# Loads of the second layer's modulation strips, moved from SyncE's queue to ScalarE's

## The chip, the cores and the metric

One core of a Trainium2 chip runs the whole program. The time is the device time of one execution in microseconds (us). The kernel before takes 1233.61 us (median of three runs, 1233.14 to 1236.70).

In the profile's rows PE is the matrix engine (TensorE), PEld its weight loads, DVE VectorE, ACT ScalarE, POOL GpSimd, SP SyncE. A name with a q behind it (SPq, ACTq) is the engine's instruction queue, where DMAs are begun.

## The reference, cut to what matters

Two decoder layers on 512 tokens of width 1024. Every layer computes six modulation vectors from one conditioning vector, and uses them as shift, scale and gate:

```
cond = jax.nn.silu(c)
for layer in range(DEPTH):
    mod = cond @ ada_w[layer] + ada_b[layer]
    sh1, sc1, g1, sh2, sc2, g2 = jnp.split(mod, 6, axis=-1)
    h = modulate(rms_norm(x, mix_norm[layer]), sh1, sc1)
    ...                                    # the layer's mixer gives y
    x = x + g1[:, None, :] * y
    h = modulate(rms_norm(x, ffn_norm[layer]), sh2, sc2)
    x = x + g2[:, None, :] * swiglu(h, ffn_w1[layer], ffn_w2[layer])
```

The second layer's mixer is a pooling mixer over four windows beside a stick-breaking attention of four heads; one output projection follows. `sh2` and `sc2` of that layer (strips 3 and 4 of its `ada_w`, each 1024 x 1024) are needed only behind the mixer, and the kernel computes them during it.

## The kernel before, in words

**The strips.** `ada_strip` (lines 249 to 265; an earlier identical definition is overwritten) walks one strip in four quarters of 256 columns. A quarter is two loads of 512 KB (line 258) into the two `ada` tiles (the pool has two), then sixteen small matmuls (line 247, eight per tile) and a copy of the sum from PSUM into half of an accumulator tile `acc` (line 264, on ScalarE). It is a generator that yields once between the loads of a quarter and its matmuls. So one step of it does: matmuls of quarter k, copy k, then the two loads of quarter k+1, which need the tiles that matmuls k have just read. Strips 3 and 4 of layer 1 give eight quarters, called pair 1 to 8 (loads), product 1 to 8 (matmuls) and copy 1 to 8 below. Copies 1, 3, 5 and 7 are the first to write a new `acc` tile; 2, 4, 6 and 8 fill the other half of one.

**The mixer's order.** `run` (lines 559 to 566) advances one main generator of twenty steps, `l1_main`, and after each of its steps one step of the side generators and then one of the strips. The first step traces the start of the attention's key projection; then `fin1` traces the broadcast of a gate (`gate_bcast`, two copies at line 380), then pair 1 is traced. Product k comes in step k+1. Attention (`sbatt`) starts in step 7: `stA` of head 0 in step 7 (with product 6), `stA` of head 1 in step 8 (ahead of product 7), `stB` of head 0 in step 9 (ahead of product 8). `stA` of a head takes twelve heap tiles: `sz`, `sa`, `sphi` and `splo`, three each.

**What sets the order of instructions.** In this stretch TensorE keeps program order, by `manual_schedule`. On the other engines a planner orders instructions while the program is built: it runs the program in a simulation and takes what is ready, earlier in the program first. Two further rules matter. `tc.keep_in_program_order` pins an instruction behind the instruction traced last before it on its own engine, in issue order alone. And tiles of a pool get their buffers in program order: the heap has 52 slots of 2 KB per partition, shared by `acc`, the pooling's and the attention's tiles, and in the program of before every one of the 970 heap tiles is begun in the order in which the program writes them first, so an instruction that begins a heap tile is not placed before those that begin earlier ones.

**Queues.** Loads of weights (`raw`, 1 MB each, lines 439 and 452, two buffers) are begun by SyncE, as are all loads of strips. ScalarE begins a load of `pool_w` (line 1714) and small ones.

Of the kernel before, what the change touches and what calls it, by code (L numbers as in the profile page):

```python
# [69 lines left out]
def trunk(ctx, tc, x, c, positions, ada_w, ada_b, ffn_w1, ffn_w2, ab_w_in, gla_gate_up,  # L70
          dsa_q_norm, dsa_k_norm, ab_w_out, cd_w_in, pool_w, cd_w_out, prm, w0, kc, out):
    nc = tc.nc
# [24 lines left out]
    def slot(dt=F32, w=512, name="s"):  # L97
        return heap.tile([P, w], dt, tag="s", name=nm(name))

    def bank(name="b"):  # L100
        return pp.tile([P, 512], F32, tag="b", name=nm(name))
# [4 lines left out]
    def ada_tile():  # L106
        return adap.tile([P, 1024], F32, tag="ada", name=nm("ada"))
# [98 lines left out]
    def ada_mm(ps, rows, j0, j1):  # L206

        for j in range(j0, j1):
            g = j % 4
            mm(ps[32 * g:32 * g + 32, :], condz[:, j, :], rows[j], start=j < 4, stop=j >= 4)  # L210

    def ada_strip(l, s, acc2, lag):
        src = ada_w[l].rearrange("(p j) n -> p j n", j=8)
        for n in range(2):
            acc = slot(name="acc")
            for q in range(2):
                c0 = s * D + n * 512 + q * 256
                rows = []
                for h in range(2):
                    rt = ada_tile().rearrange("p (j n) -> p j n", j=4)  # L220
                    tc.keep_in_program_order(nc.sync.dma_start(rt, src[:, 4 * h:4 * h + 4, c0:c0 + 256]))
                    rows += [rt[:, j] for j in range(4)]
                for _ in range(lag):
                    yield
                ps = bank("ad")
                ada_mm(ps[:, 0:256], rows, 0, 8)
                act(acc[:, q * 256:(q + 1) * 256], ps[:, 0:256], AF.Copy)
            acc2.append(acc)
# [17 lines left out]
            g = j % 4  # L246
            mm(ps[32 * g:32 * g + 32, :], condz[:, j, :], rows[j], start=j < 4, stop=j >= 4)  # L247

    def ada_strip(l, s, acc2, lag):
        src = ada_w[l].rearrange("(p j) n -> p j n", j=8)  # L250
        for n in range(2):
            acc = slot(name="acc")
            for q in range(2):
                c0 = s * D + n * 512 + q * 256
                rows = []
                for h in range(2):
                    rt = ada_tile().rearrange("p (j n) -> p j n", j=4)
                    tc.keep_in_program_order(nc.sync.dma_start(rt, src[:, 4 * h:4 * h + 4, c0:c0 + 256]))
                    rows += [rt[:, j] for j in range(4)]
                for _ in range(lag):  # L260
                    yield
                ps = bank("ad")
                ada_mm(ps[:, 0:256], rows, 0, 8)
                act(acc[:, q * 256:(q + 1) * 256], ps[:, 0:256], AF.Copy)
            acc2.append(acc)
# [293 lines left out]
    def run(main, *sides, keep=()):  # L559
        live = [iter(g) for g in sides]  # L560
        for _ in main:
            live = [g for g in live if next(g, "end") != "end"]
            for g in keep:
                next(g, None)
        while live:
            live = [g for g in live if next(g, "end") != "end"]

    def delay(g, n):
        for _ in range(n):
            yield  # L570
        yield from g
# [9 lines left out]
    def chain(*gens):  # L581
        for g in gens:
            yield from g
# [594 lines left out]
    for s_ in (2, 3, 4):  # L1178
        ada0[s_] = []
    ad = delay(chain(*(ada_strip(0, s_, ada0[s_], 1) for s_ in (2, 3, 4))), 2)  # L1180
    next(sst)
    lo_eng[0] = nc.gpsimd
# [350 lines left out]
    ada1 = {s_: [] for s_ in range(2, 6)}  # L1533
# [214 lines left out]
    def fin1():  # L1748
        gl["g1"] = gate_bcast(ada1[2])
        yield  # L1750

    def l1_main():
        yield from in_cd()
        yield from outproj_first(cd_w_out[0], 0, mixC, gl["g1"])

    lo_eng[0] = nc.gpsimd
    ad = chain(*(ada_strip(1, s_, ada1[s_], 1) for s_ in (3, 4)))
    run(l1_main(), fin1(), delay(sbatt(), 6), keep=(ad,))
    for _ in ad:
        pass  # L1760
# [37 lines left out]
```

## Time and profile before

| | us |
|---|---|
| median of three runs | 1233.61 |
| lowest, highest | 1233.14, 1236.70 |
| the profiled execution | 1229.25 |
| its span, first to last instruction | 1227.5 |
| PE busy in it | 1199.4 (98%) |
| ACT busy in it | 591.2 (48%) |
| mean granted TensorE clock | 0.993 |

The profiled execution is 4.4 us below the median of the timed runs; 1.75 us of it lie outside its span. The second layer's mixer with its strips lies at about 690 to 860 us of the span. A row of a timeline is: start us, us (from the first instruction's start to the last one's end where several are merged), engine, line, operation, output<-input, count, and in brackets the engine's idle time just before with what ended it. A queue's row is the same for begun DMAs.

### The profile page before, as it was taken

To read this page: it belongs to the slowest core of one execution; us is meant where nothing else is said; L and a number is where in the kernel's file an instruction comes from. 1 tells how busy PE (TensorE), PEld (TensorE's weight loads), DVE (VectorE), ACT (ScalarE), POOL (GpSimd) and SP (SyncE) were. 2 spreads that over 40 slices of the span, in tenths; PEclk is the share of its full clock that TensorE was granted. 3 is DMA by queue.
4 is the path that set the end of the run, shared out by engine and by line. 5 is a ranking of instruction groups with operands and counts; after the bars stand their busy time and mean duration, and the time that the engine had idled before them with its cause. 6 is when DMAs were issued, how large, how long until landed. Compare 5 with 4: busy or idle time off the path is not lost.

```text
span 1227.5 us, 19275 instructions
## 1 busy us (share of the span) xinstructions
PE 1199.4 (98%) x7584; PEld 1039.1 (85%) x7584; DVE 893.8 (73%) x1478; ACT 591.2 (48%) x1125; POOL 154.1 (13%) x153
## 2 busy tenths in 40 slices
PE   7998999999999999999999999999999999999998
PEld 3776777878899999998887877787899999998886
DVE  4487799667798787879786726765898878778333
ACT  5366347645465555553232763652465555553231
POOL 2133135500100000000000263140100000000000
PEclk8998999999999999999999999999999999999999
DMA  9544554321123423228972356322224242235221
GB/s 324 202 137 162 165 190 141 135 89 39 37 99 104 136 78 130 89 84 283 258 283 103 104 171 211 108 69 69 69 70 138 76 132 86 87 131 213 103 69 68
DMA packets 112662, 160.87 MB, mean 131 GB/s; under 512 B 7078, under 2 KB 77750, under 8 KB 112572
## 3 DMA queue, kind: packets, MB, share of 16 engines
q1 hardware_dynamic: 110544, 158.72, 39.0%
q8 instruction: 59, 0.97, 0.3%
q10 hardware_dynamic: 1964, 0.93, 0.3%
q14 instruction: 31, 0.25, 0.1%
q0 software_dynamic: 64, 0.01, 0.0%
HBM read 157.53 MB, written 2.10 MB: 130 GB/s over the span
## 4 chain that ended last, share of the span: by engine, by line
PE 83%; DVE 7%; DMA 4%; ACT 2%; issue 2%; POOL 1%; SPq 0%; ACTq 0%; DVEq 0%; POOLq 0%
PE f L1430 11%; PE f L1427 11%; PE f L1429 11%; PE f L123 4%; PE w L124 4%; PE f L124 4%; PE w L125 4%; PE f L125 4%; PE w L123 4%; PE op L124 2%; PE op L125 2%; PE op L123 2%; DMA raw<-in_ffn_w_dram 2%; PE ad L247 2%; PE f L131 2%
## 5 line engine op out<-in xcount | busy, mean ns | idle before, releaser
L119 ACT ACTIVATE whi<-raw 128x1024 fp32r<-128x1024 f32 x164 | 171.8, 1056 | 199.3 <-PE w L125 91.3
L120 DVE TENSOR_TENSOR wlo<-raw,whi 128x1024 fp32r<-128x1024 f32 x124 | 151.2, 1222 | 88.8 <-ACT whi L119 88.8
L1430 PE MATMUL f<-hhi,wlo 128*128 128x256 f32 x640 | 181.3, 283 | 0.0
L1429 PE MATMUL f<-hlo,whi 128*128 128x256 f32 x640 | 181.3, 283 | 0.0
L1427 PE MATMUL f<-hhi,whi 128*128 128x256 f32 x640 | 181.3, 283 | 0.0
L124 PE MATMUL w<-wlo,ghi 128*128 128x512 f32 x352 | 137.4, 390 | 0.5 <-DVE wlo L120 0.4
L123 PE MATMUL w<-whi,ghi 128*128 128x512 f32 x352 | 137.4, 390 | 0.3 <-ACT ghi L119 0.3
L125 PE MATMUL w<-whi,glo 128*128 128x512 f32 x352 | 137.2, 390 | 0.0
L1429 PE MATMUL f<-tlo,whi 128*128 128x256 f32 x480 | 136.0, 283 | 0.0
L1427 PE MATMUL f<-thi,whi 128*128 128x256 f32 x480 | 136.0, 283 | 0.0
L1430 PE MATMUL f<-thi,wlo 128*128 128x256 f32 x480 | 136.0, 283 | 0.0
L1434 ACT ACTIVATE e<-f 128x512 f32<-128x512 f32 x100 | 59.7, 597 | 138.9 <-PE f L1430 138.8
L1427 PEld LDWEIGHTS f<-hhi,whi 128*128 128x128 f32 x640 | 123.0, 192 | 0.0
L1429 PEld LDWEIGHTS f<-hlo,whi 128*128 128x128 f32 x640 | 123.0, 192 | 0.0
L1430 PEld LDWEIGHTS f<-hhi,wlo 128*128 128x128 f32 x640 | 123.0, 192 | 0.0
L120 POOL TENSOR_TENSOR wlo<-raw,whi 128x1024 fp32r<-128x1024 f32 x40 | 97.5, 2446 | 162.4 <-ACT whi L119 144.4
L120 DVE TENSOR_TENSOR wlo<-s,whi 128x512 fp32r<-128x512 f32 (+1 forms) x100 | 76.1, 794 | 43.9 <-ACT whi L119 43.9
L123 PE MATMUL f<-whi,hhi 128*128 128x512 f32 x240 | 96.7, 403 | 1.8 <-DVE iqr L771 1.8
L124 PE MATMUL f<-wlo,hhi 128*128 128x512 f32 x240 | 94.8, 395 | 0.1
L125 PE MATMUL f<-whi,hlo 128*128 128x512 f32 x240 | 94.4, 393 | 0.0
L1429 PEld LDWEIGHTS f<-tlo,whi 128*128 128x128 f32 x480 | 92.2, 192 | 0.0
L1430 PEld LDWEIGHTS f<-thi,wlo 128*128 128x128 f32 x480 | 92.2, 192 | 0.0
(341 smaller groups left out, 2547.8 us busy)
## 6 DMA issues: line engine op xcount, KB each, us to landing
raw<-in_ffn_w_dram SPq DMA_DIRECT2D x54, 1024.0 KB, 5.1
ada<-in_ada_w_dram SPq DMA_DIRECT2D x42, 512.0 KB, 5.2
ar<-in_ada_w_dram SPq DMA_DIRECT2D x68, 256.0 KB, 5.9
raw<-in_ab_w_in_dram SPq DMA_DIRECT2D x12, 1024.0 KB, 5.1
ada<-in_ffn_w_dram SPq DMA_DIRECT2D x24, 512.0 KB, 3.7
ar<-in_ada_w_dram SPq DMA_DIRECT2D x64, 128.0 KB, 4.0
raw<-in_cd_w_in_dram SPq DMA_DIRECT2D x8, 1024.0 KB, 5.1
x<-in_x_dram SPq DMA_DIRECT2D x16, 256.0 KB, 5.0
```

The costliest lines, as they stand in the source:

```text
L119: act(hi, src, AF.Copy)
L120: lo_eng[0].tensor_tensor(lo, src, hi, op=ALU.subtract)
L123: mm(ps, ah, bh, start=first, stop=False)
L124: mm(ps, ah, bl, start=False, stop=False)
L125: mm(ps, al, bh, start=False, stop=last)
L131: mm(ps, ah, bh, start=i == 0, stop=False)
L247: mm(ps[32 * g:32 * g + 32, :], condz[:, j, :], rows[j], start=j < 4, stop=j >= 4)
L1427: mm(ps, hi[:, k, c_], bh, start=start and k == 0 and p == 0, stop=False, skip_group_check=not start or p == 1)
L1429: mm(ps, hi[:, k, c_], bl, start=False, stop=False, skip_group_check=not start or p == 1)
L1430: mm(ps, lo[:, k, c_], bh, start=False, stop=k == 3, skip_group_check=not start or p == 1)
L1434: act(ends[name], src, fn)
```

## The change

The strip generator gets an argument that names the engine which begins its loads. For the two strips that run in the second layer's mixer it is ScalarE; the first layer's strips keep SyncE. Sixteen loads of 512 KB are concerned. Since the pin works on the load's own engine, each pair is now pinned behind the instruction traced last on ScalarE: pair 1 behind the second copy of the gate (line 380), and pair k+1 behind copy k (line 264). On SyncE the weight loads and the strips' loads no longer stand in one order.

```
-    def ada_strip(l, s, acc2, lag):
+    def ada_strip(l, s, acc2, lag, eng=nc.sync):
...
-                    tc.keep_in_program_order(nc.sync.dma_start(rt, src[:, 4 * h:4 * h + 4, c0:c0 + 256]))
+                    tc.keep_in_program_order(eng.dma_start(rt, src[:, 4 * h:4 * h + 4, c0:c0 + 256]))
...
-    ad = chain(*(ada_strip(1, s_, ada1[s_], 1) for s_ in (3, 4)))
+    ad = chain(*(ada_strip(1, s_, ada1[s_], 1, nc.scalar) for s_ in (3, 4)))
```

## Rows read from the trace of the kernel before

**Rows 1.** The page's first part: busy us, share of span, instructions of each engine.

```profile
PE 1199.4 (98%) x7584; PEld 1039.1 (85%) x7584; DVE 893.8 (73%) x1478; ACT 591.2 (48%) x1125; POOL 154.1 (13%) x153
```

**Rows 2.** Busy time by stretch, 690 to 860; the last columns are PEclk, DMA share, GB/s.

```profile
690.00:860.00 170.00, 165.18 (x871) 130.01 (x870) 98.17 (x176) 88.47 (x211) 55.35 (x47) 0.99 0.38 127
```

**Rows 3.** Waits of PE, 690 to 860: total us, times, longest us.

```profile
PE ad L247 <- DMA ada<-in_ada_w_dram: 2.6, 2, 1.7
```

**Rows 4.** Timeline of the SP queue, 690 to 830.

```profile
709.31 5.08 SPq L439 DMA_DIRECT2D raw<-in_cd_w_in_dram  x2
719.12 0.92 SPq L258 DMA_DIRECT2D ada<-in_ada_w_dram  x2
728.84 0.37 SPq L452 DMA_DIRECT2D raw<-in_cd_w_in_dram  x1
729.30 9.51 SPq L258 DMA_DIRECT2D ada<-in_ada_w_dram  x4
...
775.20 0.37 SPq L452 DMA_DIRECT2D raw<-in_cd_w_out_dram  x1
775.66 0.97 SPq L258 DMA_DIRECT2D ada<-in_ada_w_dram  x2
```

**Rows 5.** Timeline of PE, 717 to 785: products 1, 2, 3 (two rows), 7, 8.

```profile
718.42 1.07 PE L247 MATMUL ad<-ada,condz 128*32 128x256 f32 x16
...
726.88 1.07 PE L247 MATMUL ad<-ada,condz 128*32 128x256 f32 x16
...
736.14 0.64 PE L247 MATMUL ad<-ada,condz 128*32 128x256 f32 x8 [1.66 <-DMA ada<-in_ada_w_dram]
737.74 0.64 PE L247 MATMUL ad<-ada,condz 128*32 128x256 f32 x8 [0.96 <-DMA ada<-in_ada_w_dram]
...
772.07 1.07 PE L247 MATMUL ad<-ada,condz 128*32 128x256 f32 x16
...
783.91 1.07 PE L247 MATMUL ad<-ada,condz 128*32 128x256 f32 x16
```

**Rows 6.** Timeline of ACT and its queue, 710 to 790.

```profile
712.62 1.09 ACT L380 ACTIVATE gate<-gb 128x512 f32<-128x512 f32 x2 [3.63 <-PE gb L379]
...
720.90 0.36 ACT L264 ACTIVATE acc<-ad 128x256 f32<-128x256 f32 x1
...
726.26 4.21 ACT L1584 ACTIVATE sqhi<-tp,sbsc 128x128 fp32r<-128x128 f32 x16
730.25 0.50 ACT L264 ACTIVATE acc<-ad 128x256 f32<-128x256 f32 x1
...
738.45 0.46 ACTq L1714 DMA_DIRECT2D pw<-in_pool_w_dram  x1
...
781.32 0.60 ACT L1653 ACTIVATE sa<-z 128x512 f32<-128x512 f32 x1 [6.94 <-DVE sz L1652]
...
786.72 0.94 ACT L1666 ACTIVATE sphi<-sa 128x512 fp32r<-128x512 f32 x2
...
788.93 0.37 ACT L264 ACTIVATE acc<-ad 128x256 f32<-128x256 f32 x1
```

**Rows 7.** Line 258 alone, issue to landing: pairs begun at 719, 729, 755.

```profile
DMA to landing us min/median/max: 3.5/4.0/4.5
...
DMA to landing us min/median/max: 6.7/6.7/6.7
...
DMA to landing us min/median/max: 7.1/7.1/7.1
```

**Rows 8.** Busy time by stretch, 738 to 742; columns as in Rows 2.

```profile
738.00:740.00 2.00, 2.00 (x12) 1.35 (x5) 0.82 (x2) 0.38 (x1) 1.71 (x3) 0.62 0.90 266
740.00:742.00 2.00, 2.00 (x6) 1.57 (x5) 1.92 (x3) 0.00 (x0) 0.00 (x0) 0.52 0.72 206
```

**Rows 9.** Busy time by stretch, first layer, behind PE's longest idle time.

```profile
92.00:94.00 2.00, 0.00 (x0) 0.00 (x0) 1.80 (x3) 1.96 (x5) 0.00 (x0) 1.00 0.00 0
...
98.00:100.00 2.00, 1.42 (x3) 1.16 (x4) 1.90 (x3) 1.55 (x4) 0.00 (x0) 0.50 1.02 356
...
102.00:104.00 2.00, 2.00 (x7) 1.57 (x6) 1.62 (x5) 1.06 (x4) 0.00 (x0) 0.60 0.00 0
```

More of the change, by code (lines that the diff above doesn't have):

```diff
@@ L247, in ada_mm, with ada_strip @@
             mm(ps[32 * g:32 * g + 32, :], condz[:, j, :], rows[j], start=j < 4, stop=j >= 4)
-    def ada_strip(l, s, acc2, lag):
+    def ada_strip(l, s, acc2, lag, eng=nc.sync):
         src = ada_w[l].rearrange("(p j) n -> p j n", j=8)
@@ L257, in ada_strip @@
                     rt = ada_tile().rearrange("p (j n) -> p j n", j=4)
-                    tc.keep_in_program_order(nc.sync.dma_start(rt, src[:, 4 * h:4 * h + 4, c0:c0 + 256]))
+                    tc.keep_in_program_order(eng.dma_start(rt, src[:, 4 * h:4 * h + 4, c0:c0 + 256]))
                     rows += [rt[:, j] for j in range(4)]
```

## The prediction

> **What bounds the kernel now.** I read the page's first part first: PE is busy 98% of the span, ACT 48% [rows 1]. The table by stretch for the second layer's mixer shows the same there: PE 165.2 of 170 us, ACT 88.5 [rows 2]. So a microsecond in which PE stands still is lost, and one of ACT is not. Then PE's waits: the strips' loads cost it one stall, 2.6 us in two pieces [rows 3], at product 3 (736.14 and 737.74) [rows 5]. The SP queue shows why. Pair 3 is begun at 729.30, behind a 1 MB weight load at 728.84 [rows 4], although product 2 had read the tiles by 727.95 (726.88 + 1.07) [rows 5]. The stall has a tail: from 738 to 742 the granted clock is 0.62 and 0.52 of full speed [rows 8], that is 0.43 and 0.48 of two 2 us stretches, 1.8 us of work lost. Everywhere else the loads arrive in time.
>
> **What the change does, part by part.** For each quarter I compare when its loads would be begun with when PE wants them.
>
> *The issues themselves.* One load begun by ACT takes 0.46 us of its queue (line 1714) [rows 6], so sixteen take 7.4 us. ACT is idle 81.5 us of the stretch [rows 2]; I cost this at nothing. Without that cover it would be 0.9 us per pair. The same row starts at the same 738.45 as the copy ahead of it in the trace, so I take a load to begin with the start of the copy it is pinned behind, not with its end.
>
> *Pair 1* now waits for the second gate copy, which starts at about 713.1 (712.62 plus half of 1.09) [rows 6]; PE wants it at 718.42 [rows 5]. Landing takes 3.5 and 4.5 us where little else moves, 7.1 us behind a weight load [rows 7]. Alone the second load lands at 713.6 + 4.5 = 718.1: no stall. But the second of the two weight loads at 709.31 is begun at about 714.0 (709.31 + 5.08 less its own 0.37) [rows 4] and shares the DMA engines. At worst 713.6 + 7.1 = 720.7, and since product 3's second half started 1.2 us after its landing (729.87 + 6.7 = 736.6, start 737.74) [rows 4, 5, 7], 721.9 against the 718.95 when PE wants it: 2.9 us and a clock dip of 1.8, together 4.7. The pair has a start of almost 1 us on the weight load, so it is nearer to "alone": I take 0.8 (bounds 0 and 4.7; no gain, since PE waits for nothing at product 1).
>
> *Pairs 2, 4, 5, 6, 7* follow copies that run within 1.4 us of their product. Pair 2: copy at 720.90 [rows 6], landing by 721.4 + 4.5 = 725.9, wanted 726.88 [rows 5]. Pair 4 meets a weight load, the others have 7 us and more: nothing, with 0 to 1.5 us as the bound for pair 4.
>
> *Pair 3*, the one that stalls now. ACT does the sixteen `sqhi` from 726.26 to 730.47 first, so copy 2 is at 730.25 [rows 6], and the pair begins there: 0.95 us later than before, with the weight load of 728.84 still ahead. Both carry the same 2 MB through the same engines, so the last byte lands about when it does now. I take no change (bounds: −4.4, the whole stall and its tail, to +1.0).
>
> The Trainium skill bears on this: "Trainium Kernel Development and Optimization", Key Constraints, says that DMAs begun from SP, ACT and POOL run on the same 16 engines and interleave, and that issuing from several saves only the sequencer's issue time. By it the pair would overtake part of the weight load and nothing would be gained in total bytes per time; the sum stays as it is. The trace of before shows two queues in use at once only for the small load of line 1714.
>
> *Pair 8* is the term that decides. It is pinned behind copy 7. Product 7 ends at 773.14 (772.07 + 1.07) [rows 5], but copy 7 runs at 788.93, although ACT stood idle 6.94 us right before 781.32 [rows 6]. So it is not late for lack of ACT time. It is late because it begins a new `acc`, a heap tile, and heap tiles are begun in program order: `stA` of head 1, traced just ahead of product 7, begins twelve, the last ones the `splo` whose sources `sphi` are written until 787.66 (786.72 + 0.94) [rows 6]. Before, nobody waits for copy 7, and pair 8 left SP at 775.66, in time for product 8 at 783.91 [rows 4, 5]. Now pair 8 leaves at 788.93 and 789.4. With 3.5 and 4.5 us [rows 7] it lands at 792.4 and 793.9; product 8 ends at about 794.5 in place of 784.98, a loss of 9.5, and I take 9.7 for the late start seen at product 3. TensorE keeps program order, so everything behind product 8 waits (the value projection, the pooling's products, the remaining heads), and nothing behind it has slack to give back at 98%. `stA` and `stB` do not wait for product 8, so the planner has no cycle to break. Bounds: copy 7 at 787.66 and both landings 3.5: 787.66 + 0.46 + 3.5 + 0.6 = 792.2, a loss of 7.2; at the other end 788.93 + 0.46 + 7.1 + 1.2 + 0.6 = 798.3, a loss of 13.3.
>
> *The clock behind it.* After the stall that ended at 98.58 the clock is 0.50 and still 0.60 at 102 to 104 [rows 9]: 0.5 x 1.4 + 0.5 x 2 + 0.4 x 2, about 2.5 us lost. After the shorter one it was 1.8 [rows 8]. For the stall at product 8 I take 2.3 (1.8 to 3.5).
>
> *SP's queue.* Its weight loads lose the sixteen entries among them. Those loads wait for their own buffers (775.20 follows such a wait), so they start when they did: 0. The feed-forward's first loads into `ada` tiles come behind product 8 and move by as much; they are wanted after the mixer.
>
> **The sum.** 0.8 + 0 + 0 + 9.7 + 2.3 = +12.8 us. Against the profiled execution that is 1229.25 + 12.8 = 1242.0; the timed runs lie 4.4 us higher, so the forecast for their median is 1233.61 + 12.8 = 1246.4 us. Adding lower bounds without the −4.4: 0 + 7.2 + 1.8 = +9.0; with it +4.6. Upper: 4.7 + 1.5 + 1.0 + 13.3 + 3.5 = +24.
>
> **Rivals.**
> - *Faster: pair 3 freed from SP's line.* If copy 2 were placed ahead of the sixteen `sqhi`, pair 3 would leave at 727.95, before the weight load of 728.84, and the stall of 2.6 and its tail of 1.8 would go: 1233.61 − 4.4 = 1229.2. It decides from copy 2 starting before about 728.8, and needs copy 7 early as well. For it: this is the wait the trace shows. Against it: copy 2 at 730.25, and program order puts the `sqhi` first. 5%.
> - *No change.* The planner places copy 7 soon after product 7, at 773 to 776, as it does the even copies; pair 8 then leaves as before, pair 1 lands in time, pair 3 is as now: 1233 to 1235. Against it: the idle 6.94 us that copy 7 did not use. 6%.
> - *A short stall.* Copy 7 comes by 781 to 784 (fewer of head 1's tiles ahead of it), so product 8 is late by 2 to 5 us with a small dip: +3.8 to +8, about 1239. 11%.
> - *A heavier one.* Besides pair 8, pair 1 meets the weight load in full (+4.7) and pair 4 too, or ACT's new order delays weight splits: +17 to +24, about 1253. For it: two queues on the same engines at 714. 15%.
> - The forecast's mechanism with its own sizes, +8 to +17: 1242 to 1250. 63%.
>
> **How the numbers follow.** The range leaves out the two cases at the fast end (11%) and the top of the heavy one: 1238 to 1254. About 0.3% (3.7 us) is what a measurement here can tell from no change. Faster by more: the first rival, 0.05. Within: 0.06. Slower: 0.89.
>
> **What would show it.** After the change, line 258 has sixteen issues on ACTq, two of them at about 789 right with copy 7, and PE's wait for `ada` loads in the mixer grows from 2.6 us to about 13, its longest piece 8 to 10 us at product 8, followed by a stretch at half clock. If copy 7 runs before 780, or product 8 starts within 2 us of the last `stB` matmul of head 0, the main term is wrong. If product 1 waits 3 us or more, pair 1 is mis-sized. If product 3 starts without waiting, the first rival has its part.

## The result and the profile after

The changed kernel takes 1244.80 us (median of four runs, 1243.63 to 1250.87) against 1233.38 us for the kernel before beside it: a ratio of 1.0109, 95% interval 1.0079 to 1.0139, or +13.4 us (9.7 to 17.1); the two medians differ by 11.4. The forecast was +12.8 us and 1246.4 us. The total is right, but the trace shows that this is in part luck: one term that I had at nothing is a gain, another that I had at nothing is a larger loss, and only the largest term was foreseen.

The profiled execution spans 1242.7 us, 15.2 more than before. Of these, 2.6 us were there before the change could act: the gate's broadcast (line 379), which TensorE does ahead of pair 1, starts at 714.56 in place of 711.95. So 12.6 us belong to the change. The profile's page after, first part and two queues (packets, MB, share of 16 engines):

```profile
PE 1205.1 (97%) x7584; PEld 1041.1 (84%) x7584; DVE 894.1 (72%) x1478; ACT 591.0 (48%) x1125; POOL 153.0 (12%) x153
...
q1 hardware_dynamic: 102096, 150.33, 36.0%
q10 hardware_dynamic: 10412, 9.32, 2.4%
```

ACT is as busy as in [rows 1]; 8.4 MB have changed queues, 158.72 MB on q1 before and 150.33 now. PE's waits, 690 to 875 (total us, times, longest us):

```profile
PE ad L247 <- DMA ada<-in_ada_w_dram: 13.0, 4, 7.0
PE sn L1685 <- DVE mixlo L1743: 1.2, 1, 1.2
```

The second, 1.0 before, is a wait of the attention for VectorE, between products 7 and 8; it returns below. The first was 2.6 us in two pieces [rows 3]; it is now 13.0 in four. Where the four lie, in the timeline of PE after (products 1, 3, 4 in two rows, 8 in two rows):

```profile
721.03 1.07 PE L247 MATMUL ad<-ada,condz 128*32 128x256 f32 x16
...
737.03 1.07 PE L247 MATMUL ad<-ada,condz 128*32 128x256 f32 x16
...
746.12 0.64 PE L247 MATMUL ad<-ada,condz 128*32 128x256 f32 x8 [2.33 <-DMA ada<-in_ada_w_dram]
...
750.21 1.08 PE L247 MATMUL ad<-ada,condz 128*32 128x256 f32 x8 [3.45 <-DMA ada<-in_ada_w_dram]
...
796.60 1.08 PE L247 MATMUL ad<-ada,condz 128*32 128x256 f32 x8 [6.99 <-DMA ada<-in_ada_w_dram]
...
797.93 1.08 PE L247 MATMUL ad<-ada,condz 128*32 128x256 f32 x8 [0.25 <-DMA ada<-in_ada_w_dram]
```

Product 1 does not wait, nor does product 3, whose two pieces [rows 5] are gone. Product 4 waits 5.78 us (2.33 + 3.45), which it did not before, and product 8 waits 7.24. Set against the offset of 2.6, the end of product 3 comes 2.9 us earlier than before, that of product 5 3.1 later, that of product 8 11.4 later, and the span's end 12.6. Each of the three has its own cause.

**Product 3.** ACT and its queue after, 728 to 734 (`sqhi` and, below, `skhi` are high parts of the attention's split operands):

```profile
728.87 2.16 ACT L1584 ACTIVATE sqhi<-tp,sbsc 128x128 fp32r<-128x128 f32 x8
730.63 0.38 ACTq L258 DMA_DIRECT2D ada<-in_ada_w_dram  x1
730.87 0.42 ACT L1584 ACTIVATE sqhi<-tp,sbsc 128x128 fp32r<-128x128 f32 x1
731.05 0.52 ACTq L258 DMA_DIRECT2D ada<-in_ada_w_dram  x1
731.12 1.98 ACT L1584 ACTIVATE sqhi<-tp,sbsc 128x128 fp32r<-128x128 f32 x7
732.87 0.50 ACT L264 ACTIVATE acc<-ad 128x256 f32<-128x256 f32 x1
```

In ScalarE's order pair 3 stands behind copy 2. Yet its loads begin at 730.63 and 731.05, in the middle of the sixteen `sqhi`, 2.2 us before copy 2 starts at 732.87: as soon as product 2 has ended (729.49 + 1.07 = 730.56), which is what copy 2 waits for, and the loads too, for their tiles. The queue had passed copy 2 on and gone further while the engine was still at work on earlier instructions. Meanwhile SyncE's weight load, which had stood ahead of the pair [rows 4], now begins behind it (timeline of the SP queue after):

```profile
731.45 11.58 SPq L452 DMA_DIRECT2D raw<-in_cd_w_in_dram  x2
```

Pair 3's first load lands in 3.6 us where it took 6.7 [rows 7], and PE waits for neither load.

**Product 4.** The same view after, 740 to 744, and for line 119 (the split of a weight into its high part) what its queue did, with duration in ns:

```profile
740.10 0.68 ACT L1584 ACTIVATE skhi<-tp,sbsc 128x512 fp32r<-128x512 f32 x1
742.06 1.06 ACT L119 ACTIVATE whi<-raw 128x1024 fp32r<-128x1024 f32 x1 [1.27 <-issue]
742.14 0.94 ACTq L258 DMA_DIRECT2D ada<-in_ada_w_dram  x2
743.02 0.67 ACT L1584 ACTIVATE skhi<-tp,sbsc 128x512 fp32r<-128x512 f32 x1
743.10 0.58 ACTq L1714 DMA_DIRECT2D pw<-in_pool_w_dram  x1
743.59 0.37 ACT L264 ACTIVATE acc<-ad 128x256 f32<-128x256 f32 x1
```

```profile
L119 ACTq EVENT_SEMAPHORE  x1: 3574/3574/3574, 738.4 to 738.4; - x1
```

The changed loads made the planner choose another order. A weight split now stands ahead of the second `skhi`, copy 3 and pair 4. ScalarE's queue stops at it for 3.57 us, from 738.4 to 742.0, until TensorE's matmuls of line 132 are through (the last of them ends at 741.97; in the second trace of before, shown below in part, ScalarE stands idle 3.48 us before the same split, until the same line is through, but behind copy 3). Product 3 had ended at 738.10, so pair 4 could have begun there; it begins at 742.14, beside a weight load of SyncE (731.45 + 11.58 less 0.37 is 742.66) and the pooling weights, and its second load takes 7.6 us to land.

**Product 8.** The same view after, 792 to 795:

```profile
792.90 0.62 ACT L1666 ACTIVATE sphi<-sa 128x512 fp32r<-128x512 f32 x1
793.00 0.94 ACTq L258 DMA_DIRECT2D ada<-in_ada_w_dram  x2
793.42 0.41 ACT L1666 ACTIVATE sphi<-sa 128x256 fp32r<-128x256 f32 x1
...
794.04 0.37 ACT L264 ACTIVATE acc<-ad 128x256 f32<-128x256 f32 x1
```

Copy 7 runs behind the `sphi` of head 1, 15.2 us after product 7 has ended at 778.84, and pair 8 with it, here 1.0 us ahead.

**The clock** behind both stalls (busy time by stretch after, columns as in [rows 2]):

```profile
748.00:750.00 2.00, 0.00 (x0) 0.00 (x0) 1.95 (x5) 0.00 (x0) 0.00 (x0) 0.50 1.03 332
750.00:752.00 2.00, 1.79 (x10) 0.89 (x11) 0.18 (x1) 0.38 (x1) 0.00 (x0) 0.50 0.05 15
752.00:754.00 2.00, 2.00 (x7) 1.54 (x6) 0.00 (x0) 0.00 (x0) 0.00 (x0) 0.61 0.73 229
...
798.00:800.00 2.00, 2.00 (x11) 1.00 (x12) 0.00 (x0) 0.38 (x1) 0.00 (x0) 0.50 0.49 148
800.00:802.00 2.00, 2.00 (x8) 1.57 (x7) 0.00 (x0) 0.00 (x0) 0.00 (x0) 0.67 0.88 266
```

The grant falls to 0.50, the lower of the two levels (1.2 of 2.4 GHz), while PE stands, and stays there for 3 to 5 us behind the stall: to about 753.6 (752 plus 0.39 × 2 / 0.5) and 801.3. Eight matmuls of line 247 take 1.08 us there, in place of 0.64.

### The profile page after: what moved, and what is told of

Read it like the earlier page. It is cut to its first block, busy times and chain, and to the rows that moved or that the text cites. A ratio compares the mean times of both kernels' runs of the same rounds, so it can differ in the third digit from the quotient of the medians.

```text
span 1242.7 us, 19267 instructions
## 1 busy us (share of the span) xinstructions
PE 1205.1 (97%) x7584; PEld 1041.1 (84%) x7584; DVE 894.1 (72%) x1478; ACT 591.0 (48%) x1125; POOL 153.0 (12%) x153
## 3 DMA queue, kind: packets, MB, share of 16 engines
q1 hardware_dynamic: 102096, 150.33, 36.0%
## 4 chain that ended last, share of the span: by engine, by line
PE 83%; DVE 7%; DMA 4%; ACT 3%; issue 2%; SPq 1%; POOL 0%; ACTq 0%; DVEq 0%; POOLq 0%
PE f L1430 11%; PE f L1429 11%; PE f L1427 11%; PE f L123 5%; PE f L124 4%; PE f L125 4%; PE w L124 4%; PE w L125 4%; PE w L123 4%; PE op L124 2%; PE op L125 2%; PE op L123 2%; PE ad L247 2%; DMA raw<-in_ffn_w_dram 2%; PE f L131 1%
## 5 line engine op out<-in xcount | busy, mean ns | idle before, releaser
L1427 PEld LDWEIGHTS f<-thi,whi 128*128 128x128 f32 x480 | 92.2, 192 | 0.0
```

The source lines that it names most:

```text
L1427: mm(ps, hi[:, k, c_], bh, start=start and k == 0 and p == 0, stop=False, skip_group_check=not start or p == 1)
```

## The experiments

The theory: three separate terms, each to be switched alone. Their sizes by the trace: −4.4 at product 3 (the stall and tail of before), +7 to 7.5 at product 4 (3.1 + 4.4 at product 5's end), +9.5 at product 8 (12.6 − 3.1). Every experiment keeps PE's order. The timed ratios are to the kernel before on the same chip. For the traces I give two stretches, since the part ahead of the change varies from trace to trace (product 1 starts between 718.3 and 728.4 us): from the start of product 1 to the end of product 8, and from there to the span's end. Where I compare an experiment with the changed kernel I subtract their ratios; such a difference is uncertain by some 4 us either way (both intervals together), mostly from the four runs of the changed kernel.

| kernel | product 1 to 8, us | rest, us | time, ratio (95%) |
|---|---|---|---|
| before, first and second trace | 66.6, 65.5 | 442.5, 442.5 | 1.0001 (0.9984 to 1.0018) |
| after | 78.0 | 443.7 | 1.0109 (1.0079 to 1.0139) |
| pair 3 alone on ScalarE | 62.4 | 442.5 | 0.9987 (0.9974 to 1.0001) |
| pair 3 first, on SyncE | 62.1 | 443.0 | 0.9985 (0.9973 to 0.9998) |
| pair 4 alone on ScalarE | 67.4 | 443.0 | 0.9998 (0.9986 to 1.0011) |
| pair 8 alone on ScalarE | 76.0 | 443.3 | 1.0083 (1.0065 to 1.0100) |
| after, split behind pair 4 | 71.9 | 443.9 | 1.0069 (1.0053 to 1.0085) |
| after, `acc` of copy 7 early | 69.6 | 444.6 | 1.0036 (1.0023 to 1.0050) |
| after, every `acc` early | 61.4 | 444.5 | 0.9977 (0.9962 to 0.9993) |

**Pair 3 alone on ScalarE.**

```
-    def ada_strip(l, s, acc2, lag):
+    def ada_strip(l, s, acc2, lag, on_act=()):
...
-                    tc.keep_in_program_order(nc.sync.dma_start(...))
+                    tc.keep_in_program_order((nc.scalar if (s, n, q) in on_act else nc.sync).dma_start(...))
...
+    ad = chain(*(ada_strip(1, s_, ada1[s_], 1, ((3, 1, 0),)) for s_ in (3, 4)))
```

> Pair 3 alone is begun by ScalarE, the other seven pairs by SyncE. Theory: the change is three separate terms, -4.4 us at product 3, about +7 at product 4 and about +9.5 at product 8. This kernel has the first alone: pair 3 begins at about 728, ahead of the weight load, product 3 does not wait, 1233.4 - 4.4 = about 1229.0 us (ratio 0.9964). Rival A, every pair on ScalarE's queue costs the same (11.4 / 8 = 1.4 us a pair): 1234.8. Rival B, the clock dip behind product 3 comes from something else and stays: only the stall goes, 1230.8.

The first stretch is 4.1 us shorter than in the first trace of before. Again the loads run ahead of copy 2 (732.96 and 733.46 against 735.14), and product 3 does not wait. The timed gain is smaller, 1.6 us (−3.2 to +0.1): nearer to rival B than to the theory, whose −4.4 lies outside the interval as does rival A's +1.4.

This trace shows one thing more: with pair 3 alone on ScalarE, the planner already puts a weight split ahead of the second `skhi` and copy 3 (timeline of ACT). Nobody waits for it here, since pair 4 is SyncE's:

```profile
744.49 1.06 ACT L119 ACTIVATE whi<-raw 128x1024 fp32r<-128x1024 f32 x1 [1.44 <-issue]
...
746.03 0.37 ACT L264 ACTIVATE acc<-ad 128x256 f32<-128x256 f32 x1
```

**Pair 3 first, on SyncE.** Nothing on ScalarE; the weights of the value projection are issued behind pair 3.

```
-        ws = f2_weights(w, c0)
+        with tc.issue_after(last_ld[1, 3, 1, 0]) if c0 == 1536 else contextlib.nullcontext(): ws = f2_weights(w, c0)
```

> The kernel before with one thing changed: SyncE begins pair 3 ahead of the value projection's first weight load instead of behind it; nothing is begun by ScalarE. Theory: product 3 gains because its loads are begun ahead of the weight load, on whichever queue: as good as pair 3 alone on ScalarE, about -4.4 us, 1229.0 (ratio 0.9964). Rival: the gain needs the second queue (the two transfers side by side); on one queue the pair gains little or the late weight load costs it back (value projection waits): 1232 to 1236.

The SP queue of this kernel, with pair 3 ahead of the weight load:

```profile
737.51 0.92 SPq L258 DMA_DIRECT2D ada<-in_ada_w_dram  x2
738.77 0.37 SPq L452 DMA_DIRECT2D raw<-in_cd_w_in_dram  x1
```

The pair lands in 3.5 and 4.5 us, product 3 does not wait, and the time is 1.8 us less (0.3 to 3.3); the expected 4.4 is missed here too. So the gain at product 3 is a matter of order against the weight load, not of the second queue. The prediction cited the Trainium skill's page "Trainium Kernel Development and Optimization" (Key Constraints) for this: queues of several engines share the 16 DMA engines and save only issue time. The two experiments agree (62.4 and 62.1 us); what I drew from it, that the pair's landing would therefore not move, does not follow, because the queue also decides what goes first.

**Pair 4 alone on ScalarE.** The edit of pair 3 alone, with `((3, 1, 1),)`. The order of ScalarE keeps the weight split behind copy 3 and pair 4.

> Pair 4 alone is begun by ScalarE behind copy 3; the weight splits stand behind it in ScalarE's line, as in the kernel before. Theory: pair 4 on that queue costs nothing when no weight split stands ahead of copy 3; product 3 keeps its stall of 2.6 us; product 4 waits less than 1 us: ratio 1.000 (0.999 to 1.0015). Rival: pair 4 meets the weight load and the pooling weights whatever the splits do: product 4 waits 3 us or more, ratio 1.003 or more.

The time is unchanged, as the theory has it. The trace shows that the rival has a part, though: the pair begins at 740.44, right behind product 3 (late here by its usual stall), and its second load, begun at 740.99, takes 8.0 us to land, so product 4 waits a little:

```profile
748.99 0.64 PE L247 MATMUL ad<-ada,condz 128*32 128x256 f32 x8 [0.81 <-DMA ada<-in_ada_w_dram]
```

The kernel before does no better in its second trace (0.75 us at product 4). Product 4 is at the edge; the slow landing alone costs it under 1 us.

Together with pair 3 alone this shows that the loss at product 4 is no term of pair 4 by itself: pair 3 on ScalarE brings the split forward, and only a pair 4 on the same queue stands behind it.

**The split behind pair 4.** The changed kernel, with the weight split back behind the loads (`last_ld` keeps each load's instruction).

```
-        ws = f2_weights(w, c0)
+        with tc.issue_after(last_ld[1, 3, 1, 1]) if c0 == 1536 else contextlib.nullcontext(): ws = f2_weights(w, c0)
```

> The changed kernel with the value projection's weight splits issued behind pair 4's loads, as in the kernel before they stood behind copy 3; all sixteen loads stay on ScalarE. Theory: product 4 waits because a weight split that ScalarE's line now has ahead of copy 3 holds pair 4 back from about 738 to 742.1; with the split behind, pair 4 leaves at about 738 and product 4's stall (5.8 us) and its clock tail go: 1244.8 - 7 = about 1237.8 us. Rival: pair 4 is slow because it shares the DMA engines with a weight load and the pooling weights; then product 4 still waits 3 us or more, 1241 to 1245. Product 8's wait of 7 us stays in both.

Pair 4 leaves right behind product 3 and its second load lands in 4.7 us; PE does product 4 without waiting (below it, the second half of product 3):

```profile
736.72 0.37 ACTq L258 DMA_DIRECT2D ada<-in_ada_w_dram  x1
...
737.14 0.53 ACTq L258 DMA_DIRECT2D ada<-in_ada_w_dram  x1
```

```profile
742.25 1.07 PE L247 MATMUL ad<-ada,condz 128*32 128x256 f32 x16
```

```profile
736.01 0.64 PE L247 MATMUL ad<-ada,condz 128*32 128x256 f32 x8 [1.07 <-DMA ada<-in_ada_w_dram]
```

By the ratios this is 4.9 us less than the changed kernel, by the first stretch 6.1, a little short of the expected 7: product 3 waits 1.07 us in this trace. Its second load leaves 0.4 us ahead of the weight load (728.32 against 728.72) and lands only for 736.01, 7.7 us later; in the trace of after the same lead was enough (731.05 against 731.45). So the order at product 3 is won by little, and not in every trace in full. The cause of product 4's stall is shown: it is the split's place in ScalarE's line.

**Pair 8 alone on ScalarE.** The edit of pair 3 alone, with `((4, 1, 1),)`.

> Pair 8 alone is begun by ScalarE behind copy 7, the other seven pairs by SyncE. Theory: the late copy 7 is all that product 8 needs to stall; product 8 waits 7 to 8 us and a clock tail follows: the time before + 9.5 = about 1242 us (ratio 1.0077). Rival: without the other pairs copy 7 is placed elsewhere or pair 8 lands faster, a stall of 2 to 4 us, ratio 1.002 to 1.004.

+10.2 us (8.0 to 12.3); the stall (timeline of PE in this kernel):

```profile
793.26 1.08 PE L247 MATMUL ad<-ada,condz 128*32 128x256 f32 x8 [8.54 <-DMA ada<-in_ada_w_dram]
```

One pair of eight makes three quarters of the change's loss.

**The `acc` of copy 7 early.** The changed kernel with one write more, so that the heap tile of copy 7 is begun ahead of head 1's.

```
-            acc = slot(name="acc")
+            acc = slot(name="acc"); (l, s, n) == (1, 4, 1) and G.memset(acc[:, 0:1], 0.0)
```

> The changed kernel with one write more: the accumulator tile that copy 7 begins is first written (one column, by GpSimd) where it is allocated, ahead of head 1's tiles in program order. Theory: copy 7 is late because it begins a heap tile behind head 1's twelve; begun early, copy 7 runs soon after product 7, pair 8 leaves before 785, product 8 does not wait: 1244.8 - 9.5 = about 1235.3 us, with product 4's stall as it was. Rival: copy 7 is late because ScalarE's line is busy with head 1 or with its waits; then pair 8 stays late and the time is 1242 to 1245.

ACT and its queue in this kernel, 782 to 783.2: copy 7 and pair 8 come behind head 0's last `sphi`, 2.5 us after product 7 (779.28 + 1.07) in place of 15.2.

```profile
782.01 0.42 ACT L1666 ACTIVATE sphi<-sa 128x256 fp32r<-128x256 f32 x1 [1.82 <-DVE sa L1661]
782.11 0.37 ACTq L258 DMA_DIRECT2D ada<-in_ada_w_dram  x1
...
782.82 0.37 ACT L264 ACTIVATE acc<-ad 128x256 f32<-128x256 f32 x1
```

Product 8 does not wait, product 4 keeps its 5.7 us, and the time falls by 9.0 us against the changed kernel (1.0109 − 1.0036). So copy 7 was late for its heap tile's turn; ScalarE had the time. By the traces about 1.0 of the 9.0 is not product 8's: the wait for `mixlo` between products 7 and 8 falls from 1.2 us to 0.2, here and in the next experiment. Why it does was not tried.

**Every `acc` early.** The same write for all tiles of the second layer (`l and G.memset(...)`). It also moves copy 3 and pair 4 ahead of the weight splits.

> The changed kernel with every strip's accumulator tile of the second layer first written (one column, by GpSimd) where it is allocated; in its order copy 3 and pair 4 also stand ahead of the weight splits. All sixteen loads stay on ScalarE. Theory: both stalls of the changed kernel go and product 3's gain stays: about 4 us below the kernel before by the trace, ratio 0.9965 to 0.9985. Rival: sixteen loads on ScalarE's queue carry a cost of their own (issues between activations, sharing with SyncE's weight loads): ratio 1.000 or more although no product waits.

PE waits for no strip load in the mixer any more; all that its waits list from 690 to 875 is

```profile
PE so L1701 <- ACT sv L1614: 0.5, 1, 0.5
PE sn L1685 <- DVE mixlo L1743: 0.2, 1, 0.2
```

With the sixteen loads still on ScalarE the kernel is 2.8 us faster than before (0.9 to 4.7) and some 16 faster than the changed one: the rival's cost of the queue itself is not to be seen. About 0.8 of the gain is the shorter wait for `mixlo` (1.0 before). This is the fastest version run, not told apart from pair 3 first on SyncE (0.9977 and 0.9985).

**The kernel before, traced again.**

> The kernel before, unchanged, traced a second time. The traces of the first experiments give -4.2 and -4.1 us over the mixer's stretch where the timed runs give only about -1.7 (intervals to -3.3). Theory: the stall at product 3 and its clock tail repeat, product 1's start to product 8's last matmul takes again 66.2 us. Rival: the first trace caught a long stall; a usual one is shorter (65 us or less), and product 3 is worth 2 to 3 us and not 4.4.

Its ACT timeline has the weight split behind copy 3, where it holds up no load:

```profile
739.40 0.39 ACT L264 ACTIVATE acc<-ad 128x256 f32<-128x256 f32 x1
...
743.27 1.06 ACT L119 ACTIVATE whi<-raw 128x1024 fp32r<-128x1024 f32 x1 [3.48 <-PE f L132]
```

It has stalls at product 3 and a short one at product 4 (timeline of PE), and no dip behind them (busy time by stretch):

```profile
737.28 0.64 PE L247 MATMUL ad<-ada,condz 128*32 128x256 f32 x8 [1.37 <-DMA ada<-in_ada_w_dram]
...
738.70 0.64 PE L247 MATMUL ad<-ada,condz 128*32 128x256 f32 x8 [0.78 <-DMA ada<-in_ada_w_dram]
...
746.32 0.64 PE L247 MATMUL ad<-ada,condz 128*32 128x256 f32 x8 [0.75 <-DMA ada<-in_ada_w_dram]
```

```profile
740.00:742.00 2.00, 2.00 (x11) 1.64 (x10) 0.82 (x3) 0.00 (x0) 1.23 (x2) 1.00 0.76 225
```

The same stretch had 0.52 in the first trace [rows 8]. A dip follows the stall at product 3 in the first trace, in pair 4 alone and in pair 8 alone, and not here. So the tail is not always there, and product 3 is worth 2.2 us in one execution and 4.4 in another. By the measure of the expectation (start of product 1 to start of product 8's last matmul) this trace takes 65.1 us, close to the rival's 65 and not the 66.2 of the first. That goes some way to explain why the timed gains, 1.6 and 1.8, lie below the 4.1 and 4.5 that a comparison with the first trace gives. It does not explain all: against the second trace the first stretches are still 3.0 and 3.4 us shorter.

## Why the prediction was right, and where it was not

*Product 8* was the right step and the largest term: copy 7 waits for its heap tile's turn, pair 8 behind it. Of 9.7 + 2.3 forecast, the trace of after has 8.3 at the product's end and 1.2 behind it, pair 8 alone 10.2 in time. What I had too late is the load's start against its copy: it left 1.0 us before copy 7, where I had put it at the copy's start. The loss at the product's end lies inside my 7.2 to 13.3, the longest wait (7.0) below the 8 to 10 that I named as a sign. That PE's waits grew to about 13 us, as I wrote, is luck: 5.8 of the 13.0 are product 4's.

*Product 3* failed at two sentences. "I take a load to begin with the start of the copy it is pinned behind" holds for an empty line only, as in the row of line 1714 from which I took it. With sixteen `sqhi` ahead the queue went on 2.2 us before the engine. And "with the weight load of 728.84 still ahead" was wrong for the same 2.2 us: pair 3 left 0.8 us before that load. The gain that I gave as the rival "pair 3 freed" came about without the condition I set for it (copy 2 ahead of the `sqhi`). Timed it is 1.6 to 1.8 us, not the 4.4 of that rival.

*Product 4* failed at "nothing, with 0 to 1.5 us as the bound". I compared pair 4 with its copy's time in the old order of ScalarE, and took that order as given; and I costed each pair by itself. The new order, which pair 3's move brings, put a split with a 3.57 us wait ahead of pair 4. I had this in the heavier rival's list ("ACT's new order delays weight splits") but the wrong way round: the split delayed the load. By the ratios it costs 4.9 us (after less split behind) to 7.3 (`acc` of copy 7 early less every `acc` early, uncertain by 2.5).

*Product 1* (0.8) did not wait: a pair that starts ahead of a weight load was near "alone", 4.8 us to land. In the trace of `acc` of copy 7 early it waits 0.35 us. *Pairs 2, 5, 6 and 7* and *the issues themselves*: nothing, as forecast; every `acc` early has sixteen issues on ScalarE at no cost that shows.

*The sum.* By the ratios −1.6 at product 3, +4.9 to 7.3 at product 4 and +8.0 to 10.2 at product 8 make +11.3 to +15.9, and the change is +13.4 by the ratio, +11.4 by the medians. My +12.8 was too high by 0.8 at product 1, by some 1.7 at product 3 and by 2 to 4 at product 8, and too low by 5 to 7 at product 4. What I named to tell the steps apart did so: "If product 3 starts without waiting, the first rival has its part".

Two readings of mine were wrong with little weight in the sum. A grant of 0.62 loses 0.38 of its stretch and not 0.43, so the tail behind product 3 was 1.7 us, not 1.8. And there was no start 1.2 us late at product 3: the three equal figures of [rows 7] are of the first load (729.30 + 6.7 = 736.0, and product 3 started at 736.14), and the other landed as product 3's second half started, 7.9 us after its own issue (729.85 to 737.74). The 0.2 that I added at product 8 for it, and the 1.2 in the bounds, have no ground.

## What to carry to other kernels

A load that changes its queue changes neighbours: ask what it now stands behind, what it now overtakes, and which of the instructions ahead of it waits longest, for one wait holds the whole line. Where a planner sets the order, the order of before is no cover: cost the moved load against every instruction that may be put ahead of it, and the moved loads together, since one can change the order that another meets. If a load must leave early, don't hang it behind a small copy whose buffer takes its turn in a long line; a tile that is begun early, or the order on the old queue, gave the gain without the loss.

## What the runs showed of the hardware

ScalarE's queue begins DMAs ahead of activations that stand before them: 2.2 us at pair 3 in all five traces that have it on ScalarE behind the `sqhi`, 1.0 at pair 8 of after and 0.4 in pair 8 alone (789.47 against 789.85). The rows fit a hold by the last semaphore not yet met and not by the engine's backlog; that was read from them and not tested by itself.

The clock falls without a stall, too. Behind the strips' products TensorE does 32 matmuls of one column (line 270, 3.6 us). In five of the ten traces (pair 3 first on SyncE, pair 4 alone, split behind, and both with `acc` early) the grant falls during them or right behind; in five (both of before, after, pair 3 alone, pair 8 alone) it stays. The stretch behind them in the second trace of before (they end at 849.6) and, below it, the rows of every `acc` early, whose 32 matmuls end at 851.5:

```profile
849.00:853.00 4.00, 3.48 (x17) 2.35 (x17) 3.12 (x5) 0.00 (x0) 0.00 (x0) 1.00 0.39 133
```

```profile
847.00:851.00 4.00, 4.00 (x35) 3.97 (x33) 1.30 (x3) 0.93 (x2) 0.00 (x0) 0.93 0.56 174
851.00:855.00 4.00, 4.00 (x12) 3.23 (x12) 3.12 (x5) 0.00 (x0) 0.00 (x0) 0.50 0.27 92
855.00:859.00 4.00, 4.00 (x14) 3.18 (x13) 1.38 (x2) 0.71 (x2) 0.00 (x0) 0.71 0.79 258
```

PE is busy all through, and 4 × 0.07 + 4 × 0.50 + 4 × 0.29 = 3.4 us of work are lost. Runs of the kernel before lie 7 to 10 us apart (1228.58 to 1235.71 in one set of 25, 1229.11 to 1239.15 in one of 29), and the longer ones have the lower mean grant: 0.984 in the run of 1239.15, 0.993 in one of 1229.87. So the clock is the likely source of that spread; where in those runs it fell was not recorded. What decides whether it falls was not tried and stays open.
